# Rotary embedding on one core: two rows of batch 0 are rotated on their own and stored early, in float32, through SyncE

## The chip, the cores and the metric

The kernel runs on one core of a Trainium2 chip. The metric is the device time of one execution in microseconds (us). The kernel before took 318.21 us, the median of three runs, 317.97 to 318.24.

## The reference

```python
batch, seq_len, num_heads, head_dim = (8, 2048, 16, 64)      # x: float32
x1 = x[..., :head_dim // 2]
x2 = x[..., head_dim // 2:]
out1 = x1 * cos - x2 * sin          # cos, sin: (2048, 32), the same for all heads and batches
out2 = x1 * sin + x2 * cos
out  = concatenate([out1, out2], axis=-1)                    # float32
```

`x` and the result are 67.1 MB each. Every element is read once, takes part in two multiplications and an addition, and is written once.

## The kernel before

A batch is one tile of 128 partitions with J = 16 rows of 1024 elements each, in float16. GpSimd's queue loads `x` with a cast from float32 to float16 and stores with the cast back. There are five such tiles. Rows 0 and 1 (JA = 2) of each partition in batch 0 come in float32 through SyncE's queue (`head`) and are cast on ScalarE, so that work can start early. VectorE does four instructions for each batch, through a scratch tile `v` of which there is one.

```python
    JA = 2
    head = const_pool.tile([P, JA, H, D], f32)
    nc.sync.dma_start(out=head..., in_=x0[:, 0:JA, :]...)
    nc.sync.dma_start(out=sin_f, in_=...)
    nc.sync.dma_start(out=cos_f, in_=...)

    def load(b):                       # float32 -> float16, rows JA.. for batch 0, else all
        xt = io_pool.tile([P, J, H, D], f16)
        nc.gpsimd.dma_start(out=xt[:, j0:J, ...], in_=x[b]...)

    def store(b, xt):                  # float16 -> float32
        nc.gpsimd.dma_start(out=out[b]..., in_=xt)

    def rotate(xt):
        v = tmp_pool.tile([P, J, H, D], f16)
        nc.vector.tensor_mul(out=v[:, :, :, 0:Dh], in0=xt[:, :, :, Dh:D], in1=neg_b)
        nc.vector.tensor_mul(out=v[:, :, :, Dh:D], in0=xt[:, :, :, 0:Dh], in1=sin_b)
        nc.vector.tensor_mul(out=xw, in0=xw, in1=cos_b)
        nc.vector.tensor_add(out=xa, in0=xa, in1=v...)

    tiles = [load(b) for b in range(NBUF)]                # NBUF = 5
    nc.scalar.copy(out=tiles[0][:, 0:JA]..., in_=head...)
    nc.scalar.copy(out=sin_h, in_=sin_f)
    nc.scalar.mul(out=neg_h, in_=sin_f, mul=-1.0)
    nc.scalar.copy(out=cos_h, in_=cos_f)
    for b in range(B):                                    # B = 8
        rotate(tiles[b]); store(b, tiles[b])
        if b + NBUF < B: tiles.append(load(b + NBUF))
```

Of the kernel before, what the change touches and what calls it, by code (L numbers as in the profile page):

```python
# [1 line left out]

# [4 lines left out]


@with_exitstack  # L10
def kernel(
    ctx: ExitStack,
    tc: tile.TileContext,
    x: bass.AP,
    cos: bass.AP,
    sin: bass.AP,
    out: bass.AP,
):
    nc = tc.nc
    f16 = mybir.dt.float16  # L20
    f32 = mybir.dt.float32

    B, S, H, D = x.shape
    Dh = D // 2
    P = nc.NUM_PARTITIONS
    J = S // P
    NBUF = 5

    const_pool = ctx.enter_context(tc.tile_pool(name="rope_const", bufs=1))
    io_pool = ctx.enter_context(tc.tile_pool(name="rope_io", bufs=NBUF))  # L30
    tmp_pool = ctx.enter_context(tc.tile_pool(name="rope_tmp", bufs=1))

    JA = 2
    head = const_pool.tile([P, JA, H, D], f32)
    x0 = x[0].rearrange("(p j) h d -> p j (h d)", j=J)
    nc.sync.dma_start(  # L36
        out=head.rearrange("p j h d -> p (j h d)"),
        in_=x0[:, 0:JA, :].rearrange("p j f -> p (j f)"),
    )
    sin_f = const_pool.tile([P, J, Dh], f32)  # L40
    cos_f = const_pool.tile([P, J, Dh], f32)
    cos_h = const_pool.tile([P, J, Dh], f16)
    sin_h = const_pool.tile([P, J, Dh], f16)
    neg_h = const_pool.tile([P, J, Dh], f16)
    nc.sync.dma_start(out=sin_f, in_=sin.rearrange("(p j) d -> p j d", j=J))  # L45
    nc.sync.dma_start(out=cos_f, in_=cos.rearrange("(p j) d -> p j d", j=J))

    def load(b):
        xt = io_pool.tile([P, J, H, D], f16)
        j0 = JA if b == 0 else 0  # L50
        nc.gpsimd.dma_start(  # L51
            out=xt[:, j0:J, :, :].rearrange("p j h d -> p (j h d)"),
            in_=x[b].rearrange("(p j) h d -> p j (h d)", j=J)[:, j0:J, :].rearrange("p j f -> p (j f)"),
        )
        return xt

    def store(b, xt):
        nc.gpsimd.dma_start(  # L58
            out=out[b].rearrange("(p j) h d -> p (j h d)", j=J), in_=xt
        )  # L60

    def rotate(xt):
        v = tmp_pool.tile([P, J, H, D], f16)
        sin_b = sin_h.unsqueeze(2).to_broadcast([P, J, H, Dh])
        neg_b = neg_h.unsqueeze(2).to_broadcast([P, J, H, Dh])
        cos_b = cos_h.unsqueeze(2).to_broadcast([P, J, 2 * H, Dh])
        nc.vector.tensor_mul(out=v[:, :, :, 0:Dh], in0=xt[:, :, :, Dh:D], in1=neg_b)  # L67
        nc.vector.tensor_mul(out=v[:, :, :, Dh:D], in0=xt[:, :, :, 0:Dh], in1=sin_b)  # L68
        xw = xt.rearrange("p j h (e d) -> p j (h e) d", d=Dh)
        nc.vector.tensor_mul(out=xw, in0=xw, in1=cos_b)  # L70
        xa = xt.rearrange("p j h d -> p (j h d)")
        nc.vector.tensor_add(out=xa, in0=xa, in1=v.rearrange("p j h d -> p (j h d)"))  # L72

    tiles = [load(b) for b in range(NBUF)]
    nc.scalar.copy(  # L75
        out=tiles[0][:, 0:JA, :, :].rearrange("p j h d -> p (j h d)"),
        in_=head.rearrange("p j h d -> p (j h d)"),
    )
    nc.scalar.copy(out=sin_h, in_=sin_f)  # L79
    nc.scalar.mul(out=neg_h, in_=sin_f, mul=-1.0)  # L80
    nc.scalar.copy(out=cos_h, in_=cos_f)  # L81
    for b in range(B):
        rotate(tiles[b])
        store(b, tiles[b])
        if b + NBUF < B:
            tiles.append(load(b + NBUF))


# [1 line left out]
_INS = ['x', 'cos', 'sin']  # L90
_OUTS = [((8, 2048, 16, 64), 'float32')]


# [23 lines left out]
```

## Time and profile before

| | before |
|---|---|
| time, median of three runs | 318.21 us |
| span of the profiled run | 316.1 us |
| VectorE (DVE) busy | 209.2 us, 66% |
| HBM read / written | 67.63 / 67.11 MB |

These lines are from the page of the kernel before: busy tenths of VectorE and of the DMA engines in 40 equal slices of the span, and the DMA totals.

```profile
DVE  0009799999999999999879999990009993000000
...
DMA  9899999999999999999999999999999999999996
...
q0 software_dynamic: 2304, 100.14, 98.5%
q1 hardware_dynamic: 432, 1.57, 1.4%
HBM read 67.63 MB, written 67.11 MB: 426 GB/s over the span
```

VectorE has long holes. The DMA engines have none: 98.5% of their time goes to GpSimd's queue (q0) and 1.4% to SyncE's (q1). The packet records in the trace say the same by addition. This table is worked out from them; "per engine" is the sum of all durations divided by 16.

```
packets of the kernel before   count   median us   per engine us
load, float16 side 32 KB         896     2.432        137.12
first load, 28 KB                128     2.129         17.04
store, float32 side 64 KB       1024     2.449        156.59
head, 8 KB (load)                128     0.309          2.98
sin and cos, 2 KB                256     0.096          1.45
sum                                                   315.2   (span: 316.1)
```

Packets overlap a little at their ends, so the sum is no exact floor, but there is no room of any size beside it. A casting load packet is 32 KB on its float16 side and takes as long as a 64 KB store packet: the float32 side is what counts.

Now the issues. In the timeline of the kernel before, the columns are start, duration, engine, line, operation, output and input, and in brackets the idle time before and what ended it.

```profile
1.25 2.79 POOL L51 DMA_DIRECT2D xt<-in_x_dram  x5 [0.80 <-PEq L112]
...
23.65 4.43 DVE L67 TENSOR_TENSOR v<-xt,neg_h 128x8192 f16<-128x8192 f16 x1 [23.65 <-DMA xt<-in_x_dram]
...
34.16 8.69 DVE L70 TENSOR_TENSOR xt<-xt,cos_h 128x16384 f16<-128x16384 f16 x1 [1.75 <-ACT cos_h L81]
...
52.14 0.54 POOL L58 DMA_DIRECT2D out_dram<-xt  x1 [48.10 <-DVE xt L72]
...
78.12 0.54 POOL L58 DMA_DIRECT2D out_dram<-xt  x1 [25.44 <-DVE xt L72]
...
121.76 0.53 POOL L51 DMA_DIRECT2D xt<-in_x_dram  x1 [43.11 <-DMA out_dram<-xt]
...
212.86 0.53 POOL L58 DMA_DIRECT2D out_dram<-xt  x1 [12.25 <-DVE xt L72]
...
263.88 0.53 POOL L58 DMA_DIRECT2D out_dram<-xt  x1 [50.50 <-DVE xt L72]
```

Store 0 is issued at 52.1 us, but load 5, which needs its buffer, can be issued only at 121.8. In between the store's data stand behind the loads in the same queue (the ring): its first packet starts at 101.1 us, when the last packets of the loads run. Store 1 was already issued at 78.1, so the queue isn't empty when store 0 ends. That is the state of the whole kernel: something always stands in line for the 16 engines.

### The profile page before, as it was taken

What the parts mean: (1) busy time and instruction counts of PE and PEld (TensorE: products, weight loads), DVE (VectorE), ACT (ScalarE), POOL (GpSimd) and SP (SyncE); (2) the same over time, 40 slices, a digit from 0 to 9 for tenths busy, and PEclk for the clock granted to TensorE, in tenths of its full rate; (3) what the DMA queues carried; (4) which work ended last, traced back from release to release, by engine and by line L of the source; (5) the groups of instructions that cost most, each with busy time, mean ns of one, the idle gap of its engine ahead of it and who ended that gap; (6) DMA issues with size and microseconds to landing.
All of it is one profiled execution on the core that took longest, in us unless ns stands there. A gap on an engine that the chain in (4) does not pass through costs nothing.

```text
span 316.1 us, 121 instructions
## 1 busy us (share of the span) xinstructions
DVE 209.2 (66%) x32; ACT 4.9 (2%) x5; POOL 8.8 (3%) x20
## 2 busy tenths in 40 slices
DVE  0009799999999999999879999990009993000000
ACT  4100000000000000000000000000000000000000
POOL 3000000000000000010000000100000000000000
DMA  9899999999999999999999999999999999999996
GB/s 277 182 261 208 199 236 228 199 199 265 199 199 265 398 506 423 398 336 261 199 199 224 373 398 398 506 423 265 203 328 398 398 448 481 398 398 506 423 398 265
DMA packets 2736, 101.71 MB, mean 322 GB/s; under 512 B 304, under 2 KB 304, under 8 KB 560
## 3 DMA queue, kind: packets, MB, share of 16 engines
q0 software_dynamic: 2304, 100.14, 98.5%
q1 hardware_dynamic: 432, 1.57, 1.4%
HBM read 67.63 MB, written 67.11 MB: 426 GB/s over the span
## 4 chain that ended last, share of the span: by engine, by line
issue 44%; DVE 14%; another core or an unknown queue 14%; DMA 10%; POOL 1%; SPq 0%; ACT 0%; POOLq 0%
DMA cos_f<-in_cos_dram 10%; DVE xt L70 6%; DVE xt L72 6%; DVE v L67 1%; DVE v L68 1%; POOL out_dram L58 1%; POOL xt L51 0%; ACT cos_h L81 0%; POOLq L112 0%; SPq L45 0%; SPq L36 0%; POOLq L58 0%
## 5 line engine op out<-in xcount | busy, mean ns | idle before, releaser
L70 DVE TENSOR_TENSOR xt<-xt,cos_h 128x16384 f16<-128x16384 f16 x8 | 69.5, 8692 | 2.0 <-ACT cos_h L81 1.7
L67 DVE TENSOR_TENSOR v<-xt,neg_h 128x8192 f16<-128x8192 f16 x8 | 35.4, 4426 | 52.2 <-DMA xt<-in_x_dram 52.0
L72 DVE TENSOR_TENSOR xt<-xt,v 128x16384 f16<-128x16384 f16 x8 | 69.5, 8692 | 0.3
L68 DVE TENSOR_TENSOR v<-xt,sin_h 128x8192 f16<-128x8192 f16 x8 | 35.4, 4419 | 0.0
L58 POOL DMA_DIRECT2D out_dram<-xt x8 | 4.3, 535 | 136.3 <-DVE xt L72 136.3
L51 POOL DMA_DIRECT2D xt<-in_x_dram x8 | 4.4, 559 | 119.1 <-DMA out_dram<-xt 118.3
L75 ACT CAST xt<-head 128x2048 f16<-128x2048 f32 x1 | 1.9, 1897 | 3.5 <-DMA head<-in_x_dram 3.5
L75 ACT ACT_TABLE_LOAD x1 | 1.3, 1283 | 0.7 <-PEq L101 0.7
L81 ACT CAST cos_h<-cos_f 128x512 f16<-128x512 f32 x1 | 0.6, 617 | 17.7 <-DMA cos_f<-in_cos_dram 17.7
L79 ACT CAST sin_h<-sin_f 128x512 f16<-128x512 f32 x1 | 0.6, 618 | 7.2 <-DMA sin_f<-in_sin_dram 7.2
L80 ACT ACTIVATE neg_h<-sin_f 128x512 f16<-128x512 f32 x1 | 0.6, 624 | 0.0
L101 POOL MEMSET const-float32-0.0<- 128x1 f32 x1 | 0.1, 98 | 0.2 <-issue 0.2
L101 POOL MEMSET const-bfloat16-1.0<- 128x1 bf16 x1 | 0.1, 101 | 0.0
L101 POOL MEMSET const-float32-1.0<- 128x1 f32 x1 | 0.1, 98 | 0.0
L101 POOL MEMSET const-uint8-127<- 128x1 uint8 x1 | 0.1, 98 | 0.0
## 6 DMA issues: line engine op xcount, KB each, us to landing
xt<-in_x_dram POOLq DMA_DIRECT2D x7, 4096.0 KB, 41.2
xt<-in_x_dram POOLq DMA_DIRECT2D x1, 3584.0 KB, 22.3
head<-in_x_dram SPq DMA_DIRECT2D x1, 1024.0 KB, 4.8
sin_f<-in_sin_dram SPq DMA_DIRECT2D x1, 256.0 KB, 13.4
cos_f<-in_cos_dram SPq DMA_DIRECT2D x1, 256.0 KB, 31.8
out_dram<-xt POOLq DMA_DIRECT2D x8, 66.0
```

The costliest lines, as they stand in the source:

```text
L51: nc.gpsimd.dma_start(out=xt[:, j0:J, :, :].rearrange("p j h d -> p (j h d)"), in_=x[b].rearrange("(p j) h d -> p j (h d)", j=J)[:, j0:J, ...
L58: nc.gpsimd.dma_start(out=out[b].rearrange("(p j) h d -> p (j h d)", j=J), in_=xt)
L67: nc.vector.tensor_mul(out=v[:, :, :, 0:Dh], in0=xt[:, :, :, Dh:D], in1=neg_b)
L68: nc.vector.tensor_mul(out=v[:, :, :, Dh:D], in0=xt[:, :, :, 0:Dh], in1=sin_b)
L70: nc.vector.tensor_mul(out=xw, in0=xw, in1=cos_b)
L72: nc.vector.tensor_add(out=xa, in0=xa, in1=v.rearrange("p j h d -> p (j h d)"))
L75: nc.scalar.copy(out=tiles[0][:, 0:JA, :, :].rearrange("p j h d -> p (j h d)"), in_=head.rearrange("p j h d -> p (j h d)"),)
L79: nc.scalar.copy(out=sin_h, in_=sin_f)
L80: nc.scalar.mul(out=neg_h, in_=sin_f, mul=-1.0)
L81: nc.scalar.copy(out=cos_h, in_=cos_f)
L101: nc = _bacc.Bacc("TRN2", target_bir_lowering=False, num_devices=1)
```

## The change

The intent is to use the time in which the loads still run: rows 0 and 1 arrive early, so rotate them at once, cast them back into `head` and store them in float32 through SyncE's queue, which need not stand behind GpSimd's loads.

```diff
     def store(b, xt):
-        nc.gpsimd.dma_start(out=out[b]..., in_=xt)
+        j0 = JA if b == 0 else 0
+        nc.gpsimd.dma_start(out=out[b]...[:, j0:J, :]..., in_=xt[:, j0:J, :, :]...)

-    def rotate(xt):                 # all 16 rows
+    def rotate(xt, j0, j1):         # the same four instructions on rows j0 to j1

     nc.scalar.copy(out=cos_h, in_=cos_f)
+    rotate(tiles[0], 0, JA)
+    nc.scalar.copy(out=head..., in_=tiles[0][:, 0:JA, :, :]...)
+    nc.sync.dma_start(out=out[0]...[:, 0:JA, :]..., in_=head...)
     for b in range(B):
-        rotate(tiles[b])
+        rotate(tiles[b], JA if b == 0 else 0, J)
         store(b, tiles[b])
```

(The access patterns are cut at the dots.)

More of the change, by code (lines that the diff above doesn't have):

```diff
@@ L57, in store @@
     def store(b, xt):
+        j0 = JA if b == 0 else 0
         nc.gpsimd.dma_start(
-            out=out[b].rearrange("(p j) h d -> p (j h d)", j=J), in_=xt
+            out=out[b].rearrange("(p j) h d -> p j (h d)", j=J)[:, j0:J, :].rearrange("p j f -> p (j f)"),
+            in_=xt[:, j0:J, :, :].rearrange("p j h d -> p (j h d)"),
         )
-    def rotate(xt):
+    def rotate(xt, j0, j1):
         v = tmp_pool.tile([P, J, H, D], f16)
-        sin_b = sin_h.unsqueeze(2).to_broadcast([P, J, H, Dh])
-        neg_b = neg_h.unsqueeze(2).to_broadcast([P, J, H, Dh])
-        cos_b = cos_h.unsqueeze(2).to_broadcast([P, J, 2 * H, Dh])
-        nc.vector.tensor_mul(out=v[:, :, :, 0:Dh], in0=xt[:, :, :, Dh:D], in1=neg_b)
-        nc.vector.tensor_mul(out=v[:, :, :, Dh:D], in0=xt[:, :, :, 0:Dh], in1=sin_b)
-        xw = xt.rearrange("p j h (e d) -> p j (h e) d", d=Dh)
+        n = j1 - j0
+        js = slice(j0, j1)
+        sin_b = sin_h[:, js, :].unsqueeze(2).to_broadcast([P, n, H, Dh])
+        neg_b = neg_h[:, js, :].unsqueeze(2).to_broadcast([P, n, H, Dh])
+        cos_b = cos_h[:, js, :].unsqueeze(2).to_broadcast([P, n, 2 * H, Dh])
+        nc.vector.tensor_mul(out=v[:, js, :, 0:Dh], in0=xt[:, js, :, Dh:D], in1=neg_b)
+        nc.vector.tensor_mul(out=v[:, js, :, Dh:D], in0=xt[:, js, :, 0:Dh], in1=sin_b)
+        xw = xt[:, js, :, :].rearrange("p j h (e d) -> p j (h e) d", d=Dh)
         nc.vector.tensor_mul(out=xw, in0=xw, in1=cos_b)
-        xa = xt.rearrange("p j h d -> p (j h d)")
-        nc.vector.tensor_add(out=xa, in0=xa, in1=v.rearrange("p j h d -> p (j h d)"))
+        xa = xt[:, js, :, :].rearrange("p j h d -> p (j h d)")
+        nc.vector.tensor_add(out=xa, in0=xa, in1=v[:, js, :, :].rearrange("p j h d -> p (j h d)"))
     tiles = [load(b) for b in range(NBUF)]
@@ L81 @@
     nc.scalar.copy(out=cos_h, in_=cos_f)
+    rotate(tiles[0], 0, JA)
+    nc.scalar.copy(
+        out=head.rearrange("p j h d -> p (j h d)"),
+        in_=tiles[0][:, 0:JA, :, :].rearrange("p j h d -> p (j h d)"),
+    )
+    nc.sync.dma_start(
+        out=out[0].rearrange("(p j) h d -> p j (h d)", j=J)[:, 0:JA, :].rearrange("p j f -> p (j f)"),
+        in_=head.rearrange("p j h d -> p (j h d)"),
+    )
     for b in range(B):
-        rotate(tiles[b])
+        rotate(tiles[b], JA if b == 0 else 0, J)
         store(b, tiles[b])
```

## The prediction

> **What bounds the kernel now.** The 16 DMA engines. On the page their row is 9 in all slices but two, with VectorE busy 66%. The packet records add up to the whole time: a 32 KB packet of a casting load takes 2.432 us, a 64 KB packet of a store 2.447 us (26.8 GB/s per engine, on the float32 side). One engine gets 56 load packets of 2.432, 8 of the shortened first load at 2.129, 8 packets of `head` (8 KB, 0.31 to 0.38 us), 64 store packets of 2.447 and 16 sin and cos packets of 0.09: 314.3 us of a span of 316.1. Only 1.8 us is not engine work. The Trainium skill, "DMA: Bandwidth & Descriptors", section "Where 436 GB/s comes from", gives a ceiling of 435 GB/s; this trace moves 426 (HBM bytes over the span, DMA part of the page). The chain of waits names cos, VectorE and a store, but its long pieces are transfers standing in line.
>
> **What the change does.** The bytes stay the same: 1 MB of store 0's 8 MB goes as 128 float32 packets of 8 KB on SyncE's queue. The same skill page, section "Issuing engines are not separate DMA queues", says that all queues run on the same 16 engines and interleave. So the early store takes about 8 x 0.31 = 2.5 us per engine from the loads (at about 40 to 60 us), and store 0 gets 2.5 us shorter. Net 0 to +0.6 us, depending on whether an 8 KB packet costs 0.31 us (1/8 of 2.447) or 0.376 (mean of the head load).
>
> VectorE: head's third multiply needs cos_h, ready at 34.1 us. VectorE works in order and v has one buffer, so the multiplies of rows 2 to 15, which ran at 23.7 to 32.4 us, now wait behind it. Batch 0 ends near 59.5 us instead of 51.6, and later batches slip by about 8 us until VectorE next waits for a load. ScalarE gets a cast of 1.9 us.
>
> **Critical path.** None of this is on it. Store 0 was issued at 52.1 us but landed at 121.5, behind the loads in the same ring; it can be issued 8 us later for nothing. VectorE waited for load 5 until 160.1 (3.5 us idle), so the rest of the slip, about 4 us, lands on stores 4 to 6, issued at 199.6 to 212.9 while two or more transfers were queued. The last store was issued at 263.9 with over 30 us of transfers ahead of it.
>
> **Prediction.** 318.4 us, range 317.5 to 320.2; chances: faster by over 2% 0.01, within 2% 0.94, slower by over 2% 0.05.
>
> **What would show the steps right.** HBM bytes and DMA row unchanged, 426 GB/s; head's store issued at 38 to 40 us, landing about 20 us later (one small packet per large one); first VectorE work near 16 us, then a wait for cos_h until 34.1; batch 0's store issued near 60; loads 2 to 4 about 2.5 us later, store 0 landing at 121 to 122 as before; the last VectorE instruction at 264 within 2 us.
>
> **What would make it wrong.** GpSimd's issues don't stand in source order: load 5 came behind store 1. If the change reorders them so that load 5, which waits for store 0 to land, stands before store 1, the queue may run dry for an estimated 2 to 4 us at each such place: up to 10 us lost. Or small writes to HBM that mix with loads cost the engines much more than 0.38 us each, or gain by overlap.

## The result, and the profile after

The changed kernel took 318.19 us (median of six runs, 317.83 to 319.97), beside 318.21 (317.96 to 318.41, six runs) of the kernel before. The ratio is 1.0008, 95% interval 0.9985 to 1.0031. A ratio is the mean time of one kernel's fast runs over that of the other's in the same rounds, so it is not quite the ratio of the medians. One run of the changed kernel is high, 319.97; such runs are taken up under e9.

The page of the changed kernel:

```profile
DVE  0000699999999999999999999994009993000000
...
DMA  9899999999999999999999999999999999999996
...
q0 software_dynamic: 2304, 99.09, 97.7%
q1 hardware_dynamic: 576, 2.62, 2.2%
HBM read 67.63 MB, written 67.11 MB: 427 GB/s over the span
```

The DMA row and the bytes in HBM are the same. 1.05 MB has gone from q0 to q1, and the shares have moved by 0.8 points in opposite directions. VectorE starts later in full and has one hole less.

The timeline of the changed kernel, with the lines that answer to those of before:

```profile
15.13 0.69 DVE L72 TENSOR_TENSOR v<-xt,sin_h 128x1024 f16<-128x1024 f16 x1 [15.13 <-ACT sin_h L83]
...
33.95 1.23 DVE L74 TENSOR_TENSOR xt<-xt,cos_h 128x2048 f16<-128x2048 f16 x1 [17.52 <-ACT cos_h L85]
...
36.47 3.89 DVE L71 TENSOR_TENSOR v<-xt,neg_h 128x7168 f16<-128x7168 f16 x1
...
38.45 0.35 SPq L91 DMA_DIRECT2D out_dram<-head  x1
...
59.78 0.54 POOL L59 DMA_DIRECT2D out_dram<-xt  x1 [55.73 <-DVE xt L76]
...
86.02 0.54 POOL L59 DMA_DIRECT2D out_dram<-xt  x1 [25.70 <-DVE xt L76]
...
121.75 0.54 POOL L51 DMA_DIRECT2D xt<-in_x_dram  x1 [35.19 <-DMA out_dram<-xt]
...
217.31 0.53 POOL L59 DMA_DIRECT2D out_dram<-xt  x1 [16.98 <-DVE xt L76]
...
263.61 0.53 POOL L59 DMA_DIRECT2D out_dram<-xt  x1 [45.77 <-DVE xt L76]
```

Read it against before. VectorE waits 17.5 us for `cos_h`, with the multiplications of rows 2 to 15 behind that wait, and batch 0 is stored 7.6 us later (59.8 for 52.1). Store 1 is 7.9 us later. But store 0 still lands at the same moment: load 5 is issued at 121.75, before it was 121.76. Store 6 is 4.4 us later (217.3), and the last store is issued at 263.6, before it was 263.9. Each delay of VectorE has vanished where the next transfer in line decides.

The packet records of the changed kernel, worked out as before:

```
packets of the changed kernel   count   median us   per engine us
load, 32 KB                       896     2.432        136.83
first load, 28 KB                 128     2.129         17.04
store 0, 56 KB                    128     2.148         17.16
other stores, 64 KB               896     2.449        137.02
head, 8 KB (load and store)       256     0.322          5.50
sin and cos, 2 KB                 256     0.096          1.46
sum                                                    315.0
```

The head store took 5.50 less 2.98, so 2.5 us per engine, and store 0 with the other stores is 2.4 us shorter. In between, the loads end later: store 0's first packet starts at 103.4 us, before it was 101.1. So the early store pushes the loads back by 2.3 us, and the shorter store 0 makes up for it.

### The profile page after: what moved, and what is told of

It reads as the page before. It is cut to its first block, busy times and chain, and to the rows that moved or that the text cites. A ratio compares the mean times of both kernels' runs of the same rounds, so it can differ in the third digit from the quotient of the medians.

```text
span 315.8 us, 130 instructions
## 1 busy us (share of the span) xinstructions
DVE 209.7 (66%) x36; ACT 6.8 (2%) x6; POOL 8.9 (3%) x20
## 4 chain that ended last, share of the span: by engine, by line
issue 38%; another core or an unknown queue 17%; DVE 16%; DMA 10%; POOL 2%; SPq 0%; POOLq 0%; ACT 0%
DMA cos_f<-in_cos_dram 10%; DVE xt L76 6%; DVE xt L74 6%; DVE v L71 3%; DVE v L72 3%; POOL out_dram L59 1%; POOL xt L51 1%; ACT cos_h L85 0%; POOLq L125 0%; SPq L45 0%; SPq L36 0%; POOLq L59 0%; POOLq L51 0%
## 5 line engine op out<-in xcount | busy, mean ns | idle before, releaser
L74 DVE TENSOR_TENSOR xt<-xt,cos_h 128x16384 f16<-128x16384 f16 (+2 forms) x9 | 69.7, 7744 | 17.9 <-ACT cos_h L85 17.5
L76 DVE TENSOR_TENSOR xt<-xt,v 128x16384 f16<-128x16384 f16 (+2 forms) x9 | 69.7, 7744 | 0.3
L71 DVE TENSOR_TENSOR v<-xt,neg_h 128x8192 f16<-128x8192 f16 (+2 forms) x9 | 35.6, 3951 | 20.3 <-DMA xt<-in_x_dram 20.1
L72 DVE TENSOR_TENSOR v<-xt,sin_h 128x8192 f16<-128x8192 f16 (+2 forms) x9 | 35.5, 3945 | 15.1 <-ACT sin_h L83 15.1
L87 ACT CAST head<-xt 128x2048 f32<-128x2048 f16 x1 | 1.9, 1898 | 2.6 <-DVE xt L76 2.6
## 6 DMA issues: line engine op xcount, KB each, us to landing
out_dram<-head SPq DMA_DIRECT2D x1, 1024.0 KB, 27.1
```

Source lines behind the costliest of these rows:

```text
L71: nc.vector.tensor_mul(out=v[:, js, :, 0:Dh], in0=xt[:, js, :, Dh:D], in1=neg_b)
L72: nc.vector.tensor_mul(out=v[:, js, :, Dh:D], in0=xt[:, js, :, 0:Dh], in1=sin_b)
L76: nc.vector.tensor_add(out=xa, in0=xa, in1=v[:, js, :, :].rearrange("p j h d -> p (j h d)"))
L87: nc.scalar.copy(out=head.rearrange("p j h d -> p (j h d)"), in_=tiles[0][:, 0:JA, :, :].rearrange("p j h d -> p (j h d)"),)
```

## The experiments

The theory: the time is the work of the 16 DMA engines, packet after packet, and the change moves 2.5 us of it to another place in the line. The main rival: the early store does save its 2.5 us, and the 8 us slip of VectorE gives them back, so the change would win once the slip is mended. Edits are shown against the changed kernel. "Before" is the kernel before in the same rounds: its median was 317.89 us in each of the three sets (e8 and e9, the third set, ran on another chip than the rest).

| run | median us (range, runs) | ratio to before (95%) |
|---|---|---|
| e1_cos_first | 317.51 (317.37 to 319.20, 6) | 1.0001 (0.9983 to 1.0020) |
| e2_dve_late_23 | 318.07 (318.06 to 318.95, 5) | 1.0014 (1.0002 to 1.0026) |
| e3_dve_late_47 | 325.40 (325.05 to 328.10, 4) | 1.0252 (1.0222 to 1.0282) |
| e4_no_head_store (wrong) | 315.77 (315.62 to 316.22, 5) | 0.9934 (0.9922 to 0.9946) |
| e5_load5_first | 322.86 (322.55 to 323.51, 5) | 1.0160 (1.0147 to 1.0173) |
| e6_four_small | 318.06 (318.04 to 318.28, 5) | 1.0004 (0.9991 to 1.0017) |
| e7_twice | 318.04 (317.80 to 319.16, 6) | 1.0008 (0.9996 to 1.0021) |
| e8_rotate_only | 318.15 (317.86 to 318.40, 5) | 1.0006 (0.9994 to 1.0018) |
| e9_after_again | 318.21 (318.14 to 319.29, 6) | 1.0015 (1.0001 to 1.0028) |

### e1: take VectorE's slip away

```diff
+    nc.sync.dma_start(out=sin_f, ...)
+    nc.sync.dma_start(out=cos_f, ...)
     nc.sync.dma_start(out=head..., in_=x0[:, 0:JA, :]...)
-    nc.sync.dma_start(out=sin_f, ...)
-    nc.sync.dma_start(out=cos_f, ...)
```

ScalarE's casts are put into the same order.

> The changed kernel with sin and cos loaded before head, so that VectorE no longer waits for cos_h until 34 us. Theory (the sum of the engines' packets is the time): batch 0 is done some 8 us earlier, its store is issued near 51 us instead of 59.8, and the time stays 318.2 us within 0.6. Rival (the early store saves its 2.5 us, and the 8 us slip of VectorE takes them back): with the slip gone the time falls to about 315.7.

In the timeline of e1 the wait for `cos_h` is gone, the early store goes out at 31.5 us and batch 0's at 52.9:

```profile
31.52 0.34 SPq L91 DMA_DIRECT2D out_dram<-head  x1
...
52.85 0.54 POOL L59 DMA_DIRECT2D out_dram<-xt  x1 [48.81 <-DVE xt L76]
...
121.56 0.53 POOL L51 DMA_DIRECT2D xt<-in_x_dram  x1 [41.93 <-DMA out_dram<-xt]
```

The time did not fall by 2.5 us. The median, 317.51, is 0.4 us under that of before, and two of its six runs lie near 319, so the ratio is 1.0001. The other four, 317.37 to 317.52, lie below every run of the kernel before in that set (317.71 and up). In those four runs that is a gain of about 0.4 us, of which the packet records of the profiled run show a part: the 8 KB packets take 5.14 us per engine for the 5.50 of the changed kernel. The rival asked for 2.5 and fails: there is no saving of that size that a slip hides.

### e8: the rotation alone, without the early store

```diff
-    nc.scalar.copy(out=head..., in_=tiles[0][:, 0:JA]...)
-    nc.sync.dma_start(out=out[0]...[:, 0:JA, :]..., in_=head...)
```

and `store` writes all rows of batch 0 again.

> Half of the change: head is rotated on its own, as in the changed kernel, but the early store is taken away and store 0 writes all 16 rows again. VectorE slips by 8 us as in the change, the transfers are those of the kernel before. Theory: 317.9 to 318.5 us. Rival (the two halves cancel: the slip costs about 2.5 us and the early store saves as much): 320.5.

318.15 us, ratio 1.0006. In its timeline batch 0's store was issued at 62.41 us, 10.3 us later than in the kernel before, and load 5 at 121.81:

```profile
62.41 0.54 POOL L59 DMA_DIRECT2D out_dram<-xt  x1 [58.37 <-DVE xt L76]
...
121.81 0.54 POOL L51 DMA_DIRECT2D xt<-in_x_dram  x1 [32.61 <-DMA out_dram<-xt]
```

The slip by itself costs nothing that these runs resolve. With e1 this settles it: the two halves of the change don't cancel; each of them is worth about zero.

### e4: what is the early store's megabyte worth?

```diff
-    nc.sync.dma_start(out=out[0]...[:, 0:JA, :]..., in_=head...)
```

> The changed kernel without the early store: rows 0 and 1 of batch 0 are not written, the result is wrong on purpose. Theory: 1 MB less of packets, 8 x 0.315 us per engine, so 2.5 us less: 315.7 us (315.2 to 316.2), and 66.06 MB written. Rival (the early store fills gaps between the loads' packets and is free where it stands): unchanged at 318.2.

The result is wrong, since rows 0 and 1 are not written. The page of e4:

```profile
HBM read 67.63 MB, written 66.06 MB: 426 GB/s over the span
```

315.77 us, 2.1 us under the 317.89 of before, and 2.4 us under the changed kernel's 318.21 in e9, a later set on another chip with the same median of before. The theory said 2.5. The packet sums of the two profiles differ by 2.2 us: the early store's 2.5 are gone, and the loads' packets take 0.3 more (137.17 for 136.83). So a megabyte of store costs nearly its full engine time in the middle of the loads. There are no gaps that it could fill.

### e7: the change twice

```diff
     for b in range(B):
         rotate(tiles[b], JA if b == 0 else 0, J)
+        if b == 0:
+            nc.scalar.copy(out=head..., in_=tiles[0][:, JA:2*JA]...)
+            nc.sync.dma_start(out=out[0]...[:, JA:2*JA, :]..., in_=head...)
         store(b, tiles[b])      # batch 0 from row 2*JA on
```

> The change doubled: rows 2 and 3 of batch 0 also leave in float32 through SyncE, after their rotation at about 60 us, and store 0 gets 6 MB. Theory: the same bytes on the same engines, 318.2 us within 0.6. Rival (an early store through SyncE gains or loses a little each time): twice the difference of the change itself, but that was 0.0 us, so any shift over 0.6 us would speak for it.

318.04 us. In the packet records SyncE's 8 KB packets now take 8.02 us per engine, and store 0's only 14.76. Twice the change is again no change.

### e2 and e3: how late may VectorE be?

```diff
+        for _ in range(4 if j0 == JA else 1):      # e2; 7 in e3
             nc.vector.tensor_mul(out=v[:, js, :, 0:Dh], ...)
             nc.vector.tensor_mul(out=v[:, js, :, Dh:D], ...)
```

> The changed kernel with the two first multiplies of batch 0 (3.9 us each) done four times instead of once, so VectorE's batches 0 to 4 are about 23.3 us later, batch 0's store near 83 us, batch 1's near 109. Theory: that is still before the loads and store 0 have drained from the ring (about 101 and 119 us), so the time stays 318.2 within 0.6. Rival (VectorE's slip costs time at once): 8 us cost about 2.5 us, so 23 us more cost 7 or more, 325 us and up.

> The changed kernel with the two first multiplies of batch 0 done seven times, so VectorE is about 46.7 us later; batch 0's store is issued near 106 us, after the loads have drained at about 101 to 103. GpSimd's order changes by itself: load 5 now stands before store 1. Theory: two dry places, about 5 us before store 0 and about 3 us before load 5, so 324 to 328 us, far less than the 46.7 us of delay. Rival (VectorE's slip costs time at once): 318 plus 20 to 47.

In e2 batch 0's store is issued at 82.7 us and batch 1's at 109.0, 30 us later than in the kernel before:

```profile
82.72 0.54 POOL L59 DMA_DIRECT2D out_dram<-xt  x1 [78.69 <-DVE xt L77]
...
108.97 0.54 POOL L59 DMA_DIRECT2D out_dram<-xt  x1 [25.70 <-DVE xt L77]
```

The time is 318.07 us: the ratio of 1.0014 is 0.4 us, with two of its five runs near 318.9, where the rival asked for 7. In e3 the delay reaches the point where the queue runs empty. The windows of 2 and 4 us in e3 (the columns after the window: its length, the busy time of VectorE, ScalarE and GpSimd with their counts, the clock, the DMA share and GB/s):

```profile
98.00:102.00 4.00, 3.96 (x2) 0.00 (x0) 0.00 (x0) 1.00 1.22 262
102.00:106.00 4.00, 4.00 (x1) 0.00 (x0) 0.00 (x0) 1.00 0.01 0
106.00:110.00 4.00, 3.97 (x2) 0.00 (x0) 0.54 (x1) 1.00 0.53 229
...
126.00:128.00 2.00, 2.00 (x1) 0.00 (x0) 0.53 (x1) 1.00 0.02 0
```

A packet is counted in the window in which it starts, as shares over 1 show, so a share near zero means that no packet starts there. The packet records of e3 have two holes in which no engine works, 4.8 us before store 0 and 2.2 us before load 5; the mean engine, which ends a little earlier and starts a little later, rests for 5.6 and 2.5 us. The profile fell on the highest run, 328.10; the other three lie at 325.05 to 325.48 and have no profile. The median rose by 7.5 us for 46.7 us of delay. Against the kernel before VectorE has at least 30 us of slack in its first batches, and it costs time only from where the line for the DMA engines runs empty.

### e5: the risk that the prediction named

One ordering edge puts load 5 before store 1 on GpSimd (the order in which e3's instructions came by themselves).

```diff
+        if b == 1:    # store 1 after load 5, order alone, no semaphore
+            tc.add_manual_dep(st.ins, loads[5].ins.name, <no sync>, ...)
```

> The changed kernel with one ordering edge, so that on GpSimd load 5 (which waits for store 0 to land) stands before store 1. Theory: the ring is dry once, from the last packet of store 0 until load 5's first packet[...]: 2.5 to 4 us more, 320.7 to 322.2 us, with a visible hole in the DMA share near 121 us. Rival (the order doesn't matter as long as VectorE is not the limit): 318.2.

The timeline of e5 shows load 5 issued when store 0 has landed, and store 1, long ready, with store 2 only behind it:

```profile
121.88 0.53 POOL L53 DMA_DIRECT2D xt<-in_x_dram  x1 [58.95 <-DMA out_dram<-xt]
122.40 1.06 POOL L61 DMA_DIRECT2D out_dram<-xt  x2
```

The windows of e5 around it show the hole in the DMA share: from 120 to 122 us almost no packet starts (the last packets of store 0 run on until 121.0, and load 5's first starts at 123.1):

```profile
118.00:120.00 2.00, 2.00 (x2) 0.00 (x0) 0.00 (x0) 1.00 1.07 459
120.00:122.00 2.00, 2.00 (x1) 0.00 (x0) 0.12 (x1) 1.00 0.02 0
122.00:124.00 2.00, 1.97 (x2) 0.00 (x0) 1.46 (x3) 1.00 1.56 262
```

For comparison, the same windows of the kernel before, without a hole:

```profile
118.00:120.00 2.00, 2.00 (x1) 0.00 (x0) 0.00 (x0) 1.00 1.15 492
120.00:122.00 2.00, 1.97 (x2) 0.00 (x0) 0.24 (x1) 1.00 1.24 524
122.00:124.00 2.00, 2.00 (x1) 0.00 (x0) 0.29 (x1) 1.00 1.22 524
```

322.86 us, 5.0 us more than before, for one exchanged pair of issues; 2.5 to 4 was expected. In the packet records no engine works for 2.1 us, and the mean engine rests for 2.7. The remainder is in the loads' packets, 138.77 us per engine where the changed kernel has 136.83, 1.9 us more: the first 16 packets of load 5 took 3.1 us each, not 2.43, and the last 16 before store 1 took 3.7. Together that is 4.6 us, and the profiled run of e5 is 4.7 us above that of the changed kernel. Slow packets are not new: in the kernel before, the last 16 load packets before store 0 took 3.4 us each. Why they are slower was not tested.

### e6: how the two queues share an engine

```diff
-    nc.sync.dma_start(out=out[0]...[:, 0:JA, :]..., in_=head...)
+    for j in range(JA):
+        for h in (0, H // 2):
+            nc.sync.dma_start(out=out[0]...[:, j, h:h+H//2, :]..., in_=head[:, j, h:h+H//2, :]...)
```

> The changed kernel with the early store cut into four transfers of 2 KB per partition: 512 packets of 2 KB instead of 128 of 8 KB. Theory (an engine serves one small packet for each large one, and the completion takes a turn too): 4 x 9 turns of about 2.53 us, so the last of them lands about 90 us after its issue, against 27.1 us for the one transfer; engine time 32 x 0.095 = 3.0 us instead of 2.5, so the time is 318.2 to 318.9. Rival (an engine drains a whole queue at its turn): landing stays near 27 us.

318.06 us. In the packet records the four transfers, 8 packets per engine each, follow one another (first starts at 44.7, 64.7, 84.8 and 104.9 us on the span's clock). Each of the first three is spread over 20 us, so a turn takes 20 / 8 = 2.5 us, which is one 2 KB packet (0.096) and one load packet (2.43). The fourth stands beside the packets of store 0 (2.13), and its turns take 2.2 us. The last data packet started at 120.9 us, 79 us after the last issue at 42.0. That is less than the 90 expected: the completion packets mostly follow in the turn of the last data packet, so a transfer has 8 turns and not 9, and the fourth's turns are shorter. But two engines' last completion packets start at 123.2 and last for 16.9 us, to 140.1, which fits the longest landing of 98.5 us on the page; why is not known. Both are far from 27: an engine serves one small packet per turn, not the whole queue. Cutting the store into four times as many packets costs latency, and no time that shows.

### e9: the changed kernel again, and the runs near 319

> The changed kernel again, unaltered, beside the one above. Of the runs with a separate rotation and an early store so far, 7 of 28 lie about 1 us above the rest, of the kernel before none of 28. Theory: the early store isn't the cause (in two such profiles one DMA engine was already about 1 us behind when load 0 ended, before the early store was issued), so the high runs, if they come back, come in the kernel above too; the lower runs lie at 318.0. Rival (the early store causes them): high runs here and none above.

Most runs lie at 318.2, one at 319.29. The four lowest (318.14 to 318.24) are about 0.3 us above the kernel before in this set (nine of eleven runs at 317.74 to 317.96), a loss within the prediction's net 0 to 0.6 us; the first set shows none (318.19 beside 318.21). The expectation overlooked one run of the kernel before at 318.72; counted with a bar at 318.6 us, the kernels with an early store (the changed kernel in both sets, e1, e2, e6, e7) have 8 high runs of 34, and the kernel before 2 of 39, at 318.72 and 318.73. e8, without the early store, has none of 5. In the profiles of e2 and e7 that fell on such a run, one engine is behind when load 0 ends, before the early store is issued (e2: its last packet ends 1.2 us after the 113th of 128; 0.3 us in the changed kernel's 317.83 us run). The profile of e3, also on a high run, shows the same 1.2 us, and the eight other profiles show 0.7 us at most. This speaks against the early store as the cause. The counts lean the other way and are too small to decide. This stays open; it is a matter of 1 us, 0.3%.

## Why the prediction was right

The prediction was 318.4 us, in 317.5 to 320.2; measured were 318.19 and, again, 318.21.

- **What bounds the kernel.** Right. Taking 1 MB of store away (e4) takes 2.1 to 2.4 us away, near the 2.5 of its packets; taking VectorE's slip away (e1) or adding 23 us to it (e2) moves the time by about 0.4 us. The 435 GB/s that the prediction sets beside its 426 is a ceiling of the SBUF side, and this kernel's data have half their size there, in float16; the packet sum is the evidence, and the nearness of the two figures is none.
- **The price of the early store.** Right: 2.5 us per engine, 0.32 us for a packet of 8 KB, paid back by store 0. The Trainium skill, "DMA: Bandwidth & Descriptors", section "Issuing engines are not separate DMA queues", says that DMAs from all queues run on the same 16 engines; the packet sums before and after (315.2 and 315.0 us) agree.
- **VectorE's slip of 8 us and where it ends.** Right: store 0 at 59.8 us (said: near 60), store 6 later by 4.4 us (said: about 4), the last VectorE instruction ending at 263.3 (said: 264 within 2). That it is harmless was argued from the trace and is shown by e8.
- **Landing of the early store.** Issued at 38.45 us, as said, but it took 27.1 us to land, not about 20. It waited 4.2 us for its first turn (first packet at 42.6 on the span's clock), and then 8 turns passed of about 2.73 us; the prediction counted the turns only, and as 2.5 us. The slowest engine, whose last data packet started at 64.7, fits the landing at 65.5. It made no difference to the time.
- **The named risk.** GpSimd's order stayed as it was, so it didn't come true. e5 shows that it is real. The estimate of 2 to 4 us for the dry stretch fits (2.1 us for all engines, 2.7 for the mean one), but the place costs 5 us, because load packets next to it are slower, which the prediction did not have.

Where did the expected gain of the change go? There was none to have. "While the loads still run" the engines are not idle: the loads are what fills them. Finishing a megabyte of stores early delays the loads by about the time of that megabyte (2.3 us).

## What to carry to other kernels

Add up the packets' durations per DMA engine before you judge an overlap: if the sum is the span, as here, do not expect a gain from moving a transfer to another queue or to an earlier time; look for packet time that can be taken away, or for an idle stretch. In this kernel a compute engine could slip by 30 us at a cost of about 0.4 us (e2), as long as the line for the DMA engines did not run empty. So guard the order of the issues: a load that waits for a store must not stand before a store that is ready (e5: 5 us for one exchange).

## What the Trainium skill lacked or had wrong

- "DMA: Bandwidth & Descriptors", section "Queues, rings and completion order", says that an engine drains a whole packet, typically about 9 to 17 descriptors, from one queue before it turns to the next. Here the engines did take turns, but SyncE's queue moved one row of 2 KB or 8 KB per turn (two of 8 KB in the first turn of most engines) against one 32 KB row (float16 side) of a load: 8 rows of 2 KB took 20 us in e6. If a row is one descriptor, which the trace does not say, the typical packet is not what stands here. A small transfer beside large ones is therefore slow to land (27.1 us for 1 MB) though it costs only 2.5 us of engine time.
- The same page, sections "SWDGE vs HWDGE vs iDMA" and "Rules for kernel authors", says which queue can cast, but not what a cast costs: here a casting load runs at the pace of its float32 side (2.432 us for 32 KB of float16, against 2.449 for 64 KB of float32 in a store), so loading to float16 saved no DMA time.
- "HBM Reference", section "Specifications (TRN2)", gives about 425 GB/s for a core that streams alone, without saying whether loads and stores mixed reach it; here they do, with 426 GB/s over the whole span.
- No page that was read says that load packets next to an empty stretch or before a store can be slower: in e5 the first 16 after the hole took 3.1 us and the last 16 before store 1 took 3.7, against 2.43, which is 1.9 us per engine beyond the hole itself.
